# A gated feed-forward block in a transformer layer: seven products for four pairs of weight row tiles instead of three, two of the sums by accumulating transfers, activations through DRAM

## The chip, the cores and the metric

The kernel runs on one core of a Trainium2 chip. The metric is the device time of one execution in microseconds (us); lower is better. The time of the kernel before is the median of three runs.

## The reference, cut to what matters

One layer on 256 tokens of width 2048: a mixer of four head groups, then a gated feed-forward network of 5632 hidden columns. All arrays are float32.

```python
h = rms_norm(x, norm_mix_pre)
mix = hybrid_mixer(h, ...)
x = x + rms_norm(mix @ w_out, norm_mix_post)
h = rms_norm(x, norm_ffn_pre)
f = (silu(h @ w_gate) * (h @ w_up)) @ w_down
x = x + rms_norm(f, norm_ffn_post)
```

The change lies in `h @ w_gate` and `h @ w_up` (2048 x 5632 each) and in how the hidden activations reach `@ w_down`.

## The kernel before, in words

**Stages.** The input projections, the mixers and the output projection take the first 416 us. A stage for the first 512 columns of gate and up follows (the `gemm` call of L892, accumulators `ff`). Then a loop over ten *blocks* (L925) does the other 512-column slices of gate and up, and a last stage (from L946) does the down projection in two halves of 22 units. A kernel-wide library orders each engine's instructions by priority in the order of the code and by when it expects a buffer to be free; on the chip each engine works its own list strictly in that order and waits on semaphores.

**One float32 product is three matmuls.** A weight tile of 128 x 1024 (two pieces of 512 columns) is loaded into a buffer `raw`. ScalarE casts it to a rounded part `hi` (L768), and VectorE subtracts to get the rest, `lo` (L769); this is `split_to`, called by `split_new` (L799). `mm1` (L813) then issues three matmuls per product: activation times `hi`, activation times `lo`, activation remainder times `hi` (L815, L816, L817), each with 512 moving columns. There are five `raw` buffers and four each of `hi` and `lo`.

**A unit is two row tiles of the weights.** For a block, the 2048 rows are 16 row tiles, that is eight units `u` = 0 to 7. A unit's packed weights are four pieces: gate of row tile 0 (called a), up of row tile 0 (b), up of row tile 1 (d), gate of row tile 1 (c). `load4` (L786) loads pairs of them. With two halves of 128 tokens, a unit is a 2 x 2 by 2 x 2 block product: `eight` (L822) does it with eight products, of 3 matmuls each.

**`fifteen` (L833) does units u and u+1 together with 15 products:** seven for unit u by the scheme of Strassen and Winograd, and eight for u+1 in two parts of four (`part8`, L841). Seven products need sums of weights: `ta` = (a+b, d+b) by VectorE (L850), `tb` = (a+b+d, a+b+d+c) by two more adds (L855, L856), and sums of activations `cmb`, made once per unit before the loop (`combine_hs`, L884). The products go to four PSUM banks that hold the corrections (`m1`, `m6`, `m7`, `q5`) and four that hold results (`b2`, `b3`, `b4`, `b8`). Splits in the order in which they are made: a and d (w0), first half of u+1 (w0e), `ta` (wa), second half of u+1 (w1), c (wc), `tb` (wb). So `fifteen` makes five and a half splits of 1024 columns and three adds, where two calls of `eight` make four splits.

**A block before** is `eight` of unit 0, `fifteen` of units 1 and 2, 3 and 4, 5 and 6 (`S_UNITS`, L39), `sums` (L866), `eight` of unit 7: 8 + 15 + 15 + 15 + 8 = 61 products. `sums` combines the correction banks in SBUF tiles `g` and `v`: one copy on ScalarE (L868) and four adds on VectorE (L869 to L872). Then `turn` (L905) transposes the previous block's hidden activations on TensorE (8 transposes, accumulators `fT`, L911) and copies them to an SBUF tile `ft` (L912). `join` (L874) adds the result banks to `g` and `v` with four VectorE instructions (L876, L877, L879, L880). Last, ScalarE applies SiLU (L942) and VectorE multiplies gate by up (L943), two instructions each. Eleven `ft` tiles stay in SBUF until the down stage splits them (`hidden`, L914).

All loads are issued by the queue of SyncE (SP), in program order. The tiles `ta`, `tb`, `g`, `v`, `ft`, `cmb`, `hs` share one pool of 34 buffers of 4 KB per partition (tag `t`).

Of the kernel before, what the change touches and what calls it, by code (L numbers as in the profile page):

```python
# [10 lines left out]
F32 = mybir.dt.float32  # L11
# [27 lines left out]
S_UNITS = (1, 3, 5)  # L39
# [61 lines left out]
def block_kernel(ctx: ExitStack, tc: tile.TileContext, I, out):  # L101
# [655 lines left out]
    def spill(h):  # L757
        for q in range(2):
            nc.sync.dma_start(x_mid[:, 2 * h + q, :], xr[h][q])
# [73 lines left out]
    def fifteen(m, src, i, x, u, cmb, last, end=False):  # L833
# [69 lines left out]
    ft, fs, fcmb = [], {}, {}  # L903

    def turn(b, f):  # L905

        ft.append(T([P, 4, S], f"ft{b}"))
        for h in range(2):
# [3 lines left out]
            nc.scalar.copy(ft[b][:, :, h * P:(h + 1) * P], ps.rearrange("p (a b) -> p a b", a=4))  # L912

    def hidden(u):  # L914

        if u in fs:
            return
        v = ft[u // 2][:, 2 * (u % 2):2 * (u % 2) + 2, :]
        fs[u] = operand("fs", 2)[0]
        split_to(fs[u][:, :, 0, :], fs[u][:, :, 1, :], v)  # L920
        if u in S_DOWN[0] + S_DOWN[1]:
            fcmb[u] = combine(v)

    f = sg
    for b in range(1, FFB):  # L925
        m = {}
        g, v = T([P, 2, 512], "g"), T([P, 2, 512], "v")
        for u in range(KT // CK):
            i = (b - 1) * (KT // CK) + u
            if u in S_UNITS:  # L930
                fifteen(m, I["w_gu"], i, hs, u, cmb[u], u == S_UNITS[-1], u == KT // CK - 2)
            elif u - 1 not in S_UNITS:
                eight(m, I["w_gu"], i, hs, u, u == KT // CK - 1)
            if u == 4 and b == FFB - 1:
                hidden(0)
            if u == S_UNITS[-1]:
# [120 lines left out]
```

## Time and profile before

| what | value |
|---|---|
| median of three runs | 1135.75 us (1135.08 to 1139.37) |
| the profiled execution's own time | 1137.63 us |
| its span, first to last instruction | 1135.4 us |
| mean granted clock of TensorE | 0.996 of full |
| gate and up loop, ten blocks | from about 464.6 to 888.5 us of the span |
| down projection and end | from 888.5 us on |

A profile shows one execution: busy time of each engine, in what order instructions ran, what ended each wait, and what the DMA queues moved. A matmul's own duration is longer than the distance to the next one, since matmuls overlap; the distance is the price.

### The profile page before, as it was taken

To read this page: it belongs to the slowest core of one execution; us is meant where nothing else is said; L and a number is where in the kernel's file an instruction comes from. 1 tells how busy PE (TensorE), PEld (TensorE's weight loads), DVE (VectorE), ACT (ScalarE), POOL (GpSimd) and SP (SyncE) were. 2 spreads that over 40 slices of the span, in tenths; PEclk is the share of its full clock that TensorE was granted. 3 is DMA by queue.
4 is the path that set the end of the run, shared out by engine and by line. 5 is a ranking of instruction groups with operands and counts; after the bars stand their busy time and mean duration, and the time that the engine had idled before them with its cause. 6 is when DMAs were issued, how large, how long until landed. Compare 5 with 4: busy or idle time off the path is not lost.

```text
span 1135.4 us, 14600 instructions
## 1 busy us (share of the span) xinstructions
PE 1118.2 (98%) x5341; PEld 932.1 (82%) x5341; DVE 863.9 (76%) x1185; ACT 613.5 (54%) x846; POOL 14.2 (1%) x37
## 2 busy tenths in 40 slices
PE   9999999999999999999999999999999999999996
PEld 7787888888888887888888888888888788888885
DVE  6555647787565579688988988988988887778765
ACT  6644435565444556455555555555555665555542
POOL 0000000000000010000000000000000000000000
PEclk9999999999999999999999999999999999999999
DMA  8974454554556686466666666556556666666664
GB/s 276 326 231 149 131 160 129 196 186 157 158 183 194 199 314 223 137 197 204 190 200 209 192 192 214 189 190 220 186 188 222 188 189 198 201 206 208 206 218 149
DMA packets 75944, 224.36 MB, mean 198 GB/s; under 512 B 8032, under 2 KB 8544, under 8 KB 75872
## 3 DMA queue, kind: packets, MB, share of 16 engines
q1 hardware_dynamic: 75728, 223.42, 61.0%
q8 instruction: 42, 0.69, 0.2%
q14 instruction: 30, 0.25, 0.1%
q10 hardware_dynamic: 144, 0.01, 0.0%
HBM read 219.20 MB, written 4.19 MB: 197 GB/s over the span
## 4 chain that ended last, share of the span: by engine, by line
PE 91%; DVE 3%; DMA 3%; ACT 2%; issue 1%; POOL 0%; SPq 0%; DVEq 0%; POOLq 0%; ACTq 0%
PE b L815 15%; PE b L817 15%; PE b L816 15%; PE sx L223 3%; PE wo L197 3%; PE wo L198 3%; PE wo L200 3%; PE m L817 2%; PE m L815 2%; PE m L816 2%; PE dk L223 2%; PE lk L223 2%; PE rqk L223 2%; PE dq L223 2%; DMA raw<-in_w_in 2%; PE lq L223 1%
## 5 line engine op out<-in xcount | busy, mean ns | idle before, releaser
L768 ACT CAST hi<-raw 128x1024 fp32r<-128x1024 f32 x248 | 242.0, 983 | 173.6 <-PE b L817 143.6
L769 DVE TENSOR_TENSOR lo<-raw,hi 128x1024 fp32r<-128x1024 f32 x248 | 275.5, 1131 | 63.8 <-ACT hi L768 59.4
L183 DVE TENSOR_TENSOR lo<-raw,hi 128x1024 fp32r<-128x1024 f32 (+3 forms) x154 | 175.5, 1154 | 113.1 <-ACT hi L182 112.8
L182 ACT CAST hi<-raw 128x1024 fp32r<-128x1024 f32 (+3 forms) x154 | 150.6, 994 | 127.9 <-PE wo L200 32.1
L815 PE MATMUL b<-hi,hs 128*128 128x512 f32 x460 | 179.8, 391 | 0.0
L817 PE MATMUL b<-hi,hs 128*128 128x512 f32 x460 | 179.1, 389 | 0.0
L816 PE MATMUL b<-lo,hs 128*128 128x512 f32 x460 | 179.0, 389 | 0.0
L815 PE MATMUL b<-hi,fs 128*128 128x512 f32 x286 | 112.2, 392 | 1.8 <-ACT fs L768 1.8
L816 PE MATMUL b<-lo,fs 128*128 128x512 f32 x286 | 111.9, 391 | 0.0
L817 PE MATMUL b<-hi,fs 128*128 128x512 f32 x286 | 111.7, 391 | 0.0
L817 PEld LDWEIGHTS b<-hi,hs 128*128 128x128 f32 x460 | 86.3, 188 | 18.1
L816 PEld LDWEIGHTS b<-lo,hs 128*128 128x128 f32 x460 | 86.4, 188 | 17.7
L815 PEld LDWEIGHTS b<-hi,hs 128*128 128x128 f32 x460 | 86.4, 188 | 17.6
L768 ACT CAST hi<-tb 128x1024 fp32r<-128x1024 f32 x41 | 43.3, 1055 | 85.0 <-PE b L817 85.0
L769 DVE TENSOR_TENSOR lo<-tb,hi 128x1024 fp32r<-128x1024 f32 x41 | 50.0, 1220 | 31.6 <-ACT hi L768 31.3
L815 PEld LDWEIGHTS b<-hi,fs 128*128 128x128 f32 x286 | 54.0, 189 | 13.3 <-ACT fs L768 2.0
L816 PEld LDWEIGHTS b<-lo,fs 128*128 128x128 f32 x286 | 54.1, 189 | 11.4
L817 PEld LDWEIGHTS b<-hi,fs 128*128 128x128 f32 x286 | 54.1, 189 | 11.2
L768 ACT CAST hi<-ta 128x1024 fp32r<-128x1024 f32 x41 | 43.1, 1052 | 29.9 <-PE b L817 25.6
L769 DVE TENSOR_TENSOR lo<-ta,hi 128x1024 fp32r<-128x1024 f32 x41 | 49.9, 1217 | 6.1 <-ACT hi L768 6.0
L850 DVE TENSOR_TENSOR ta<-raw 128x1024 f32<-128x1024 f32 x41 | 49.9, 1216 | 4.3 <-DMA raw<-in_w_gu 4.1
L197 PE MATMUL wo<-hi,ms 128*128 128x512 f32 x128 | 50.0, 390 | 0.0
(378 smaller groups left out, 2017.7 us busy)
## 6 DMA issues: line engine op xcount, KB each, us to landing
raw<-in_w_gu SPq DMA_DIRECT2D x160, 512.0 KB, 4.7
raw<-in_w_down SPq DMA_DIRECT2D x88, 512.0 KB, 4.4
raw<-in_w_in SPq DMA_DIRECT2D x78, 512.0 KB, 4.6
raw<-in_w_out SPq DMA_DIRECT2D x32, 512.0 KB, 3.5
raw<-in_w_in SPq DMA_DIRECT2D x16, 384.0 KB, 3.1
raw<-in_w_g SPq DMA_DIRECT2D x8, 512.0 KB, 4.7
raw<-in_w_u SPq DMA_DIRECT2D x8, 512.0 KB, 4.6
raw<-in_w_in SPq DMA_DIRECT2D x8, 264.0 KB, 2.7
```

Source lines behind the costliest of these rows:

```text
L182: nc.scalar.copy(hi[:, k, :n], r3[:, k, :])
L183: nc.vector.tensor_tensor(lo[:, k, :n], r3[:, k, :], hi[:, k, :n].bitcast(F32), ALU.subtract)
L197: nc.tensor.matmul(d[:, :n], lhsT=a, rhs=hi[:, kt % CK, :n], start=first, stop=False)
L198: nc.tensor.matmul(d[:, :n], lhsT=a, rhs=lo[:, kt % CK, :n], start=False, stop=False)
L200: nc.tensor.matmul(d[:, :n], lhsT=b, rhs=hi[:, kt % CK, :n], start=False, stop=last)
L223: nc.tensor.matmul(o, lhsT=l, rhs=r, start=kt == 0 and i == 0, stop=kt == n_kt - 1 and i == 1)
L768: nc.scalar.copy(hi, v)
L769: nc.vector.tensor_tensor(lo, v, hi.bitcast(F32), ALU.subtract)
L815: nc.tensor.matmul(o, lhsT=xa, rhs=hi, start=first, stop=False)
L816: nc.tensor.matmul(o, lhsT=xa, rhs=lo, start=False, stop=False)
L817: nc.tensor.matmul(o, lhsT=xb, rhs=hi, start=False, stop=last)
L850: nc.vector.tensor_tensor(ta, ad, bc_[:, 0:1, :].to_broadcast([P, 2, 512]), ALU.add)
```

## The change

The change does five things.

1. `S_UNITS` becomes (0, 2, 4, 6): every block is four calls of `fifteen`, 60 products, and there is no call of `eight`. One more `cmb` is made before the loop.
2. For units 2 and 6 (`S_DMA`), `by_dma` makes `ta` by transfers: SP loads a and b into a buffer `ta`, then GpSimd's queue issues a transfer of b and d that adds to it. VectorE's add for `ta` goes away there. Since only a, d and c are then needed as such, the load of b and c becomes a load of c alone (256 KB).
3. In the block's last `fifteen`, the correction products come first, then `sums`, then the last four products of unit 7.
4. `turn` writes its transposed tile to a DRAM tensor `f_mid` by a transfer on ScalarE's queue, and `hidden` loads it back on SP and splits both units of it at once.
5. `spill`, which writes the residual to DRAM, is issued by ScalarE instead of SP.

```diff
-S_UNITS = (1, 3, 5)
+S_UNITS = (0, 2, 4, 6)
+S_DMA = (2, 6)
...
-            nc.sync.dma_start(x_mid[:, 2 * h + q, :], xr[h][q])
+            nc.scalar.dma_start(x_mid[:, 2 * h + q, :], xr[h][q])
...
+    def by_dma(src, i):
+        n = 4 * P * 512
+        w = src[i * n:(i + 1) * n].rearrange("(p c n) -> p c n", p=P, c=4)
+        t = T([P, 2, 512], "ta")
+        nc.sync.dma_start(t, w[:, 0:2, :])
+        nc.gpsimd.dma_start(t, w[:, 1:3, :], accum_op=ALU.add)
+        return t
...
-    def fifteen(m, src, i, x, u, cmb, last, end=False):
+    def fifteen(m, src, i, x, u, cmb, last, end=None, ta=None):
...
-        ad, bc_ = load4(src, i, slice(0, 3, 2), slice(1, 4, 2))
-        ta, tb = T([P, 2, 512], "ta"), T([P, 2, 512], "tb")
-        nc.vector.tensor_tensor(ta, ad, bc_[:, 0:1, :].to_broadcast([P, 2, 512]), ALU.add)
+        tb = T([P, 2, 512], "tb")
+        if ta is None:
+            ad, bc_ = load4(src, i, slice(0, 3, 2), slice(1, 4, 2))
+            c_ = bc_[:, 1:2, :]
+            ta = T([P, 2, 512], "ta")
+            nc.vector.tensor_tensor(ta, ad, bc_[:, 0:1, :].to_broadcast([P, 2, 512]), ALU.add)
+        else:
+            ad, c_ = load4(src, i, slice(0, 3, 2), slice(3, 4))
         r0, r1 = load4(src, i + 1, slice(0, 2), slice(2, 4))
         w0 = split_new(ad)
         prod(("m1", xpart(x, u, 0, 0), w0, 0), ("b3", s(3), w0, 1))
         w0e = split_new(r0)
         nc.vector.tensor_tensor(tb[:, 0, :], ta[:, 0, :], ad[:, 1, :], ALU.add)
-        nc.vector.tensor_tensor(tb[:, 1, :], tb[:, 0, :], bc_[:, 1, :], ALU.add)
-        part8(w0e)
+        nc.vector.tensor_tensor(tb[:, 1, :], tb[:, 0, :], c_[:, 0, :], ALU.add)
+        part8(0, w0e)
         wa = split_new(ta)
-        w1 = split_new(r1)
+        if end is None:
+            w1 = split_new(r1)
         prod(("q5", s(0), wa, 0), ("m7", s(2), wa, 1))
-        part8(w1)
-        wc = split_new(bc_[:, 1:2, :])
+        if end is None:
+            part8(1, w1)
+        wc = split_new(c_)
         wb = split_new(tb)
         prod(("b2", xpart(x, u, 1, 0), wc, 0), ("m6", s(1), wb, 0), ("b4", xpart(x, u, 1, 1), wb, 1))
+        if end is not None:
+            w1 = split_new(r1)
+            end()
+            part8(1, w1, True)
...
+    f_mid = dram.tile([P, FFB, 4, S], F32, name="f_mid")
...
+        nc.scalar.dma_start(f_mid[:, b], t)
...
+    def hidden(b):
+        t = T([P, 4, S], f"fl{b}")
+        nc.sync.dma_start(t, f_mid[:, b])
+        for k in range(2):
...
-        for u in range(KT // CK):
-            i = (b - 1) * (KT // CK) + u
-            if u in S_UNITS:
-                fifteen(m, I["w_gu"], i, hs, u, cmb[u], u == S_UNITS[-1], u == KT // CK - 2)
-            elif u - 1 not in S_UNITS:
-                eight(m, I["w_gu"], i, hs, u, u == KT // CK - 1)
+        i = (b - 1) * (KT // CK)
+        tas = {u: by_dma(I["w_gu"], i + u) for u in S_DMA}
+        for u in S_UNITS:
+            end = u == S_UNITS[-1]
+            fifteen(m, I["w_gu"], i + u, hs, u, cmb[u], end, (lambda: sums(m, g, v)) if end else None, tas.get(u))
...
-            for k in (u + 1, u + 2):
-                if k < n_u:
-                    hidden(k)
+            if q == 0 and u % 2 == 0 and u // 2 + 1 < FFB:
+                hidden(u // 2 + 1)
```

Three places in the instruction lists show what moved. The first is VectorE's list at the end of a block, from the first add of `sums` on (`lo<-raw,hi` is the subtraction of a split; `m`, `q` and `b` are the banks). Before:

```order
L869 TENSOR_TENSOR v_5275<-g_5274,m_182_5395 128x512
L769 TENSOR_TENSOR lo<-raw,hi 128x1024
L870 TENSOR_TENSOR g_5274<-v_5275,m_182_5368 128x512
L769 TENSOR_TENSOR lo<-raw,hi 128x1024
L871 TENSOR_TENSOR v_5275<-v_5275,q_182_5364 128x512
L872 TENSOR_TENSOR v_5275<-q_182_5364,g_5274 128x512
L876 TENSOR_TENSOR g_5274<-g_5274,b_180_5288 128x512
L877 TENSOR_TENSOR v_5275<-b_180_5292,v_5275 128x512
L879 TENSOR_TENSOR g_5274<-g_5274,b_180_5302 128x512
L880 TENSOR_TENSOR v_5275<-v_5275,b_180_5306 128x512
L850 TENSOR_TENSOR ta_5674<-raw 128x1024
L943 SCALAR_TENSOR_TENSOR v_5275<-v_5275,rsf_r,g_5274 128x512 x2
```

With the change (L890 to L893 are `sums`, L897 to L901 `join`, L965 the multiplication, L863 the add for `ta`, L770 the subtraction):

```order
L890 TENSOR_TENSOR v_5325<-g_5324,m_193_5415 128x512
L770 TENSOR_TENSOR lo<-raw,hi 128x1024
L891 TENSOR_TENSOR g_5324<-v_5325,m_193_5388 128x512
L897 TENSOR_TENSOR g_5324<-g_5324,b_193_5361 128x512
L892 TENSOR_TENSOR v_5325<-v_5325,q_193_5384 128x512
L893 TENSOR_TENSOR v_5325<-q_193_5384,g_5324 128x512
L898 TENSOR_TENSOR v_5325<-b_193_5351,v_5325 128x512
L900 TENSOR_TENSOR g_5324<-g_5324,b_193_5368 128x512
L901 TENSOR_TENSOR v_5325<-v_5325,b_193_5372 128x512
L965 SCALAR_TENSOR_TENSOR v_5325<-v_5325,rsf_r,g_5324 128x512 x2
L863 TENSOR_TENSOR ta_5704<-raw 128x1024
L870 TENSOR_TENSOR tb_5699<-ta_5704,raw 128x512
```

Both lists run through `sums`, `join` and the multiplication. Before, the next block's `ta` belongs to units 1 and 2; with the change it belongs to units 0 and 1, and the next split behind it is that of `ta`.

The second place is TensorE's list at the same boundary with the change, from the transposes on (L933; L816 to L818 are the three matmuls of a product):

```order
L933 MATMUL fT_127_5303<-ident,v_4591 128x128 x4
L933 MATMUL fT_128_5309<-ident,v_4591 128x128 x4
L816 MATMUL m_193_5347<-hi,hs_3717 128x512
L817 MATMUL m_193_5347<-lo,hs_3717 128x512
L818 MATMUL m_193_5347<-hi,hs_3717 128x512
L816 MATMUL b_193_5351<-hi,cmb_4059 128x512
L817 MATMUL b_193_5351<-lo,cmb_4059 128x512
L818 MATMUL b_193_5351<-hi,cmb_4059 128x512
L816 MATMUL b_193_5351<-hi,hs_3718 128x512
L817 MATMUL b_193_5351<-lo,hs_3718 128x512
L816 MATMUL b_193_5361<-hi,hs_3718 128x512
L817 MATMUL b_193_5361<-lo,hs_3718 128x512
```

After the transposes come `m1` and `b3` of unit 0 and four products of unit 1, 18 matmuls in all, and then the first matmul that reads `hi` of `ta`. Before, 24 matmuls of unit 0 stand behind the transposes, then 18 of units 1 and 2, and only then the first that reads `hi` of `ta`.

The third is SP's list with the change, around the loads into `ta` for the DMA sums (L839; `ta` number 5326 is unit 2's, 5329 unit 6's of one block):

```order
L796 DMA raw<-in_w_gu 128x1024 x2
L796 DMA raw<-in_w_gu 128x2x512 x2
L796 DMA raw<-in_w_gu 128x1024 x2
L796 DMA raw<-in_w_gu 128x2x512
L796 DMA raw<-in_w_gu 128x512
L839 DMA ta_5326<-in_w_gu 128x1024
L839 DMA ta_5329<-in_w_gu 128x1024
L796 DMA raw<-in_w_gu 128x1024 x2
L796 DMA raw<-in_w_gu 128x2x512 x2
```

The code asks for both at the start of the block. They stand behind five and a half loads of the block: all four of units 0 and 1, and the loads of a, d and of c of unit 2.

## Rows read from the trace of the kernel before

**Rows 1.** the page, busy time of each engine, and the granted clock in 40 slices

```profile
PE 1118.2 (98%) x5341; PEld 932.1 (82%) x5341; DVE 863.9 (76%) x1185; ACT 613.5 (54%) x846; POOL 14.2 (1%) x37
PEclk9999999999999999999999999999999999999999
```

**Rows 2.** the chain that ended last: start us, length us, what (transposes between blocks)

```profile
506.15 0.87 PE fT L911 x8
548.53 0.87 PE fT L911 x8
...
887.65 0.87 PE fT L911 x8
```

**Rows 3.** busy time by stretch; columns by engine, then clock, DMA share, GB/s

```profile
core 0: us, PE busy (x) PEld busy (x) DVE busy (x) ACT busy (x) POOL busy (x), PEclk, DMA share, GB/s
591.80:634.18 42.38, 42.38 (x193) 35.18 (x192) 37.86 (x46) 24.19 (x28) 0.00 (x0) 1.00 0.63 198
```

**Rows 4.** TensorE in order of time at a block boundary: start us, us, what

```profile
590.77 1.03 PE L911 MATMUL fT<-ident,v 128*128 128x128 f32 x8
591.56 0.48 PE L815 MATMUL b<-hi,hs 128*128 128x512 f32 x1
591.88 0.40 PE L816 MATMUL b<-lo,hs 128*128 128x512 f32 x1
592.11 0.39 PE L817 MATMUL b<-hi,hs 128*128 128x512 f32 x1
```

**Rows 5.** VectorE in order of time at two boundaries, same columns

```profile
593.90 1.41 DVE L943 SCALAR_TENSOR_TENSOR v<-v,rsf_r,g 128x512 f32<-128x512 f32 x2
595.23 2.35 DVE L769 TENSOR_TENSOR lo<-raw,hi 128x1024 fp32r<-128x1024 f32 x2
...
628.08 0.68 DVE L869 TENSOR_TENSOR v<-g,m 128x512 f32<-128x512 f32 x1
628.68 1.22 DVE L769 TENSOR_TENSOR lo<-raw,hi 128x1024 fp32r<-128x1024 f32 x1
629.82 0.68 DVE L870 TENSOR_TENSOR g<-v,m 128x512 f32<-128x512 f32 x1
...
634.54 0.68 DVE L880 TENSOR_TENSOR v<-v,b 128x512 f32<-128x512 f32 x1
635.14 1.22 DVE L850 TENSOR_TENSOR ta<-raw 128x1024 f32<-128x1024 f32 x1
```

**Rows 6.** group by line, three blocks: count, busy us, mean ns, idle before

```profile
L768 ACT CAST hi<-ta 128x1024 fp32r<-128x1024 f32 x9 | 9.5, 1052 | 5.3 <-PE b L817 5.3
```

**Rows 7.** VectorE later in the block: idle time before a row and its releaser

```profile
622.87 1.23 DVE L769 TENSOR_TENSOR lo<-tb,hi 128x1024 fp32r<-128x1024 f32 x1 [2.02 <-ACT hi L768]
626.94 1.23 DVE L769 TENSOR_TENSOR lo<-raw,hi 128x1024 fp32r<-128x1024 f32 x1 [1.49 <-ACT hi L768]
```

**Rows 8.** TensorE after its two longest waits before the last stage

```profile
38.33 0.39 PE L223 MATMUL lq<-xs,lo 128*128 128x256 f32 x1 [2.01 <-DVE lo L183]
896.68 0.50 PE L815 MATMUL b<-hi,fs 128*128 128x512 f32 x1 [1.80 <-ACT fs L768]
898.24 0.63 PE L815 MATMUL b<-hi,fs 128*128 128x512 f32 x1
...
901.23 0.52 PE L816 MATMUL b<-lo,fs 128*128 128x512 f32 x1
```

**Rows 9.** stretches behind those two waits, columns as in rows 3

```profile
38.00:40.00 2.00, 1.67 (x10) 1.49 (x11) 1.24 (x2) 1.26 (x3) 0.00 (x0) 1.00 0.74 223
898.00:900.00 2.00, 2.00 (x7) 1.50 (x6) 2.00 (x4) 1.23 (x3) 0.00 (x0) 0.52 0.87 307
```

**Rows 10.** the page, DMA issues: transfer, queue, count, size, us to landing

```profile
raw<-in_w_gu SPq DMA_DIRECT2D x160, 512.0 KB, 4.7
x_mid<-xr SPq DMA_DIRECT2D x4, 512.0 KB, 7.0
```

More of the change, by code (lines that the diff above doesn't have):

```diff
@@ L839, in prod, with part8 @@
                 mm1(m, name, xa, xb, hi[:, k, :], lo[:, k, :], last and name[0] != "b")
-        def part8(w):
-            k = 0 if w is w0e else 1
+        def part8(k, w, fin=False):
             for h in range(2):
@@ L845, in part8 @@
                 for j in range(2):
-                    mm1(m, names[j ^ k], *xpart(x, u + 1, k, h), w[0][:, j, :], w[1][:, j, :], end and k == 1)
-        ad, bc_ = load4(src, i, slice(0, 3, 2), slice(1, 4, 2))
-        ta, tb = T([P, 2, 512], "ta"), T([P, 2, 512], "tb")
-        nc.vector.tensor_tensor(ta, ad, bc_[:, 0:1, :].to_broadcast([P, 2, 512]), ALU.add)
+                    mm1(m, names[j ^ k], *xpart(x, u + 1, k, h), w[0][:, j, :], w[1][:, j, :], fin)
+        tb = T([P, 2, 512], "tb")
[6 more added lines that the diff above has]
+            ad, c_ = load4(src, i, slice(0, 3, 2), slice(3, 4))
         r0, r1 = load4(src, i + 1, slice(0, 2), slice(2, 4))
@@ L901, in block_kernel @@
         nc.vector.scalar_tensor_tensor(sg[h], accs[h][1], rs_f[h][:, 0:1], sg[h], ALU.mult, ALU.mult)
-    ft, fs, fcmb = [], {}, {}
+    fs, fcmb = {}, {}
+    f_mid = dram.tile([P, FFB, 4, S], F32, name="f_mid")
     def turn(b, f):
-        ft.append(T([P, 4, S], f"ft{b}"))
+        t = T([P, 4, S], f"ft{b}")
         for h in range(2):
@@ L911, in turn @@
                 nc.tensor.transpose(ps[:, j * P:(j + 1) * P], f[h][:, j * P:(j + 1) * P], ident)
[L912 to L922, printed above, removed]
+            nc.scalar.copy(t[:, :, h * P:(h + 1) * P], ps.rearrange("p (a b) -> p a b", a=4))
+        nc.scalar.dma_start(f_mid[:, b], t)
[3 more added lines that the diff above has]
+        for k in range(2):
+            u = 2 * b + k
+            v = t[:, 2 * k:2 * k + 2, :]
+            fs[u] = operand("fs", 2)[0]
+            split_to(fs[u][:, :, 0, :], fs[u][:, :, 1, :], v)
+            if u in S_DOWN[0] + S_DOWN[1]:
+                fcmb[u] = combine(v)
     f = sg
@@ L927, in block_kernel @@
         g, v = T([P, 2, 512], "g"), T([P, 2, 512], "v")
-        for u in range(KT // CK):
-            i = (b - 1) * (KT // CK) + u
-            if u in S_UNITS:
-                fifteen(m, I["w_gu"], i, hs, u, cmb[u], u == S_UNITS[-1], u == KT // CK - 2)
-            elif u - 1 not in S_UNITS:
-                eight(m, I["w_gu"], i, hs, u, u == KT // CK - 1)
+        i = (b - 1) * (KT // CK)
[3 more added lines that the diff above has]
+            fifteen(m, I["w_gu"], i + u, hs, u, cmb[u], end, (lambda: sums(m, g, v)) if end else None, tas.get(u))
             if u == 4 and b == FFB - 1:
                 hidden(0)
-            if u == S_UNITS[-1]:
-                sums(m, g, v)
         turn(b - 1, f)
```

## Prediction

> **What bounds the kernel now.** I read the page first: TensorE is busy 98% of the span at full clock, VectorE 76% [rows 1]. Then the chain of waits. In the gate and up loop it is TensorE alone, and its transposes, one set per block, come at an even step: 506.15 and 887.65 are the first and the last of ten, so a block takes 381.5 / 9 = 42.39 us [rows 2]. Next, busy time by block: TensorE has no idle time, VectorE works 37.86 of 42.38 us, and the DMA engines are busy 0.63 of the time at 198 GB/s [rows 3]. A block holds 61 x 3 = 183 matmuls and the transposes (0.87 us), so a matmul costs (42.39 - 0.87) / 183 = 0.227 us. So a product less is worth time only if nothing makes TensorE wait. What decides is therefore the order of VectorE at the block boundary, read from the timeline [rows 4, 5]. VectorE waits for ScalarE's casts late in a block, up to 2.02 us at a time [rows 7]: it is ahead there and has slack. At the boundary it has none.
>
> **What the change saves.** One product per block: 3 x 0.227 = 0.68 us, times ten blocks **-6.8 us**.
>
> **What it adds on VectorE.** Per block one add for `ta` less (three become two; 1.14 us is the step from one 1024-column row to the next, 628.68 to 629.82 [rows 5]), two adds for `tb` more (0.60 us each, the step of 512 columns, 634.54 to 635.14 [rows 5]), and 22 splits for 20.5. That is -1.14 + 1.20 + 1.71 = +1.8 us. VectorE then works about 39.6 of 41.7 us. As a sum this still fits, so I cost it at nothing by itself; its cover is TensorE's 41.7 us, and if that went, all 1.8 us a block would show.
>
> **The block boundary, step by step.** Take as zero the start of the transposes. With the change TensorE has behind them 18 matmuls whose operands are split before the boundary. Transposes 0.79 us (590.77 to 591.56 [rows 4]) plus 18 x 0.227 plus 0.09 for the slow first one makes 4.95 us of cover. The next matmul reads `hi` of `ta`.
>
> When is that ready? Backwards from zero there are 21 matmuls (c and `tb` nine, unit 7's last four products twelve) behind the last product that reads `ta` of unit 6. That product ends at -21 x 0.227 + 0.16 = -4.6 us (0.16: a matmul runs 0.39 and steps 0.227 [rows 4]). Its `hi` buffer is the one that the next block's first cast needs, as there are four and three splits lie between. So: cast 1.06 us [rows 6] to -3.5, its subtraction 1.14 to -2.35. Only now does VectorE reach `sums`. Its list, each entry by its step: `sums` and `join` 8 x 0.60, one subtraction among them 1.14, the two of the multiplication 1.33 (593.90 to 595.23), the add for `ta` 1.22 [rows 5]. Sum 8.5: `ta` is there at 6.15 us. Its cast ends at 7.2, with hand-overs of some 0.06 each at about 7.4. **TensorE waits 7.4 - 4.95 = 2.45 us.** Then five matmuls read `hi` parts only, but one of them needs the cast behind (8.4 us): 0.5 us more. Together 2.95 us. Before, 42 matmuls lie between the transposes and the first read of `ta`, 9.5 us of cover, and nothing waits.
>
> There are nine such boundaries (into blocks 2 to 10): 9 x 2.95 = **+26.5 us**. The first block starts behind the stage before, without this queue of adds.
>
> **The clock.** Rows show that a wait of TensorE can cost twice. After a wait of 1.80 us it ran from 898.24 to 901.23 with seven steps of 0.43 us [rows 8], at a granted clock of 0.52, the 1.2 GHz level [rows 9]: some eight matmuls lost 0.2 us each, 1.6 us. It had run without a wait before. After a wait of 2.01 us at 36 us the clock stayed at 1.00, 2.4 GHz [rows 8, 9]. So one wait in two. Bounds: 0 and 9 x 1.6 = 14.4 us. The waits here are longer, so I take six of nine: **+9.6 us**.
>
> **The transfers into `ta`.** SP can issue the load of c of unit 2 when a `raw` buffer comes free, by my count the one whose subtraction lies between the first two adds of `sums`, which ends at -0.6 us; the two loads into `ta` follow at about 0. A load of 512 KB lands in 4.7 us [rows 10]. VectorE wants unit 2's `ta` for `tb`, behind the two `tb` adds and the splits of `ta`, of unit 1's second half, of c and `tb` and of unit 2's first: from 7.4 us 4 x 1.14 + 0.60, near 12.7. That leaves 8.0 us for the accumulating transfer. No row shows one. Lower bound: as a plain load, 4.7 us, no wait. Upper: a load and a store in sequence, 4.7 + 7.0 = 11.7 us [rows 10], a wait of 3.7 us in each of ten blocks, +37 us. I take the lower, since it is the same 512 KB from the same tensor.
> The Trainium skill (DMA: Bandwidth & Descriptors, section on the anatomy of a DMA on the GpSimd path) gives 2.0 us plus the bytes at 436 GB/s, an estimate of 3.2 us; by it nothing waits either.
>
> These transfers also share the DMA engines. A block moves 16 pieces of 512 KB now; with the change 14 + 1 (two halves of c), two plain and two accumulating loads and the `f_mid` store, 20, or 22 if accumulating counts twice. Busy share 0.63 x 20/16 x 42.4/45.3 = 0.74, up to 0.81. Loads will land later. VectorE runs without slack for the first half of a block, so a late load there shows. Bounds 0 and, with the upper bound above, inside the same 37 us; I take 0.5 us a block: **+5 us**.
>
> **At nothing, or nearly.** The 11 stores and loads through `f_mid` are spread under TensorE's work; the store's issue is on ScalarE, which is busy 24 of 42 us [rows 3]. `spill` moves four issues to ScalarE once. The down stage keeps its instruction counts; at its start TensorE waits 1.80 us already [rows 8], and splitting two units at once lengthens that: **+1 us**.
>
> **Sum:** -6.8 + 26.5 + 9.6 + 5 + 1 = +35.3 us. The profiled execution took 1137.63 us (span 1135.4, 2.2 us around it), 1.9 above the median of 1135.75. From it the sum gives 1172.9, against the median **1171 us**.
>
> **The rivals.**
> - *The boundary wait alone* (clock stays up, loads in time): -6.8 + 26.5 + 1 = +20.7, 1156 us. For it: the clock stayed up after 2.01 us.
> - *The accumulating transfers are late* and VectorE stands at unit 2's `tb` in each block. Price up to 37 us besides the boundary's, in place of the 5: it decides from 8.0 us issue to landing on. 1185 to 1210 us. For it: a store takes 7.0 us, the transfer must read what it changes, and loads queue behind it. The Trainium skill (the same page, on issuing engines not being separate DMA queues) speaks for this one: transfers from every queue run on the same 16 engines, so a sum moved off VectorE is paid there. No run here shows it yet.
> - *The boundary is covered* and the product is gained: 1129 us. Place: VectorE's queue of `sums`, `join` and `ta`. It decides from `ta`'s cast being done 4.95 us after the transposes start, 2.45 us earlier than I count. For it: before, VectorE is ahead at the end of a block [rows 7]. Against: its list is worked strictly in order, and the adds of `join` wait for TensorE's last products.
> - *Gain and wait cancel*: a boundary wait of 0.7 us instead of 2.95. Within 5 us of before.
>
> **How the numbers follow.** Forecast 0.46, boundary alone 0.20, late transfers 0.27, covered 0.04, cancelled 0.03. A measurement of this kernel tells about 0.5%, 5.7 us, from no change: covered is faster (0.04), cancelled the same (0.03), the rest slower (0.93). The range reaches from just under the boundary alone, 1152, into the late transfers, 1205; it leaves out the two small cases and the upper end of the late transfers.
>
> **What would show it.** A step between transposes of about 45 to 47 us. In the timeline, TensorE idle 2 to 3 us behind 18 matmuls after the transposes, released by ScalarE's cast of `ta`. Granted clock of about half in some stretches behind it. VectorE without idle time until mid-block. In the DMA issues, the accumulating transfer under 8 us and no wait of VectorE on it; a long wait of `tb` on a DMA into `ta` would mean late transfers. I am wrong if TensorE shows no wait at the boundary, or if the loss lies in the down stage.

## The result and the profile after

The changed kernel takes **1179.27 us** (median of four runs, 1175.02 to 1180.65), the kernel before 1136.46 us beside it: ratio **1.0376, interval 1.0357 to 1.0394**. The forecast was 1171 us in a range of 1152 to 1205. The profiled execution is the shortest of the four, 1175.02 us with a span of 1173.2 us, so what its trace shows (37.8 us more span than before) is a little less than what the medians differ by.

The page first: busy times, the queue of the accumulating transfers, the shares of the chain that ended last, and the DMA issues (transfer, queue, count, size, us to landing).

```profile
PE 1128.5 (96%) x5311; PEld 928.1 (79%) x5311; DVE 888.3 (76%) x1221; ACT 629.7 (54%) x867; POOL 31.9 (3%) x57
...
q0 software_dynamic: 2880, 10.49, 5.0%
...
PE 73%; DVE 12%; DMA 8%; ACT 3%; issue 3%; POOL 0%; DVEq 0%; SPq 0%; POOLq 0%; ACTq 0%
...
raw<-in_w_gu SPq DMA_DIRECT2D x140, 512.0 KB, 4.6
...
ta<-in_w_gu SPq DMA_DIRECT2D x20, 512.0 KB, 5.9
ta<-in_w_gu POOLq DMA_DIRECT2D x20, 512.0 KB, 7.8
...
f_mid<-ft ACTq DMA_DIRECT2D x11, 512.0 KB, 6.1
```

TensorE falls from 98% to 96% [rows 1], and the chain now runs 12% over VectorE and 8% over transfers. Where? The transposes (line 933 now), first and tenth set:

```profile
504.76 0.49 PE L933 MATMUL fT<-ident,sg 128*128 128x128 f32 x3
...
923.74 0.71 PE L933 MATMUL fT<-ident,v 128*128 128x128 f32 x5
```

Nine blocks take 418.98 us, 46.55 each in place of 42.39 [rows 2]: +37.5 us. Ahead of the first transposes it is 1.2 us less, behind the last 1.5 us more. The loss lies in the blocks.

The first of the ten blocks has no such boundary ahead of it. From its first matmul to the transposes it takes 40.81 us (463.95 to 504.76), and 41.49 before (464.51 to 505.99). So there the saved product shows at once, 0.68 us:

```profile
463.95 0.39 PE L816 MATMUL m<-hi,hs 128*128 128x512 f32 x1
```

```profile
464.51 0.39 PE L815 MATMUL b<-hi,hs 128*128 128x512 f32 x1
...
505.99 0.49 PE L911 MATMUL fT<-ident,sg 128*128 128x128 f32 x3
```

One boundary in order of time, TensorE, then VectorE and ScalarE (lines 816 to 818 are the three matmuls of a product, 769 the cast, 770 its subtraction, 863 the add that makes `ta`, 965 the multiplication that closes a block; square brackets: idle before, and what ended it). The transposes start at 551.14.

```profile
555.94 0.40 PE L818 MATMUL b<-hi,hs 128*128 128x512 f32 x1
558.40 0.51 PE L816 MATMUL q<-hi,cmb 128*128 128x512 f32 x1 [2.06 <-ACT hi L769]
558.74 0.39 PE L816 MATMUL m<-hi,cmb 128*128 128x512 f32 x1
559.35 0.98 PE L816 MATMUL b<-hi,hs 128*128 128x512 f32 x3 [0.22 <-ACT hi L769]
```

```profile
554.12 0.68 DVE L901 TENSOR_TENSOR v<-v,b 128x512 f32<-128x512 f32 x1
554.72 1.41 DVE L965 SCALAR_TENSOR_TENSOR v<-v,rsf_r,g 128x512 f32<-128x512 f32 x2
556.05 1.22 DVE L863 TENSOR_TENSOR ta<-raw 128x1024 f32<-128x1024 f32 x1
...
557.30 1.05 ACT L769 CAST hi<-ta 128x1024 fp32r<-128x1024 f32 x1 [2.33 <-DVE ta L863]
```

This is the queue that the prediction counted: `join`, multiplication, `ta`, cast. VectorE's rows follow each other without a hole, and TensorE stands 2.46 us from start to start where a step is 0.23. Before, VectorE went from the multiplication to the remainder of a cast and nobody waited [rows 4, 5].

The waits (who, line, for whom: us in total, times, longest) and two blocks as stretches (columns as in [rows 3]), with 2 us of the second:

```profile
ACT hi L769 <- DMA raw<-in_w_gu: 28.6, 13, 4.7
...
PE q L816 <- ACT hi L769: 18.8, 9, 2.1
...
DVE tb L870 <- DMA ta<-in_w_gu: 7.6, 3, 5.8
```

```profile
551.14:598.10 46.96, 43.56 (x189) 34.15 (x188) 39.39 (x46) 25.54 (x29) 1.74 (x2) 1.00 0.72 224
598.10:644.02 45.92, 43.80 (x189) 35.43 (x188) 39.48 (x46) 25.75 (x29) 1.74 (x2) 0.96 0.73 229
606.00:608.00 2.00, 1.97 (x5) 1.40 (x5) 2.00 (x3) 1.72 (x3) 0.87 (x1) 0.50 0.97 182
```

Nine waits of TensorE at nine boundaries. VectorE waits for a sum made by a transfer three times, but 5.8 of the 7.6 us are one wait in the first block, where nothing is lost. And two blocks lose time in different ways: the second runs a while at half clock (0.50, the 1.2 GHz level) behind its boundary; the first doesn't, and still takes 1 us more. The chain of waits through the first one says what binds there instead:

```profile
556.13 1.14 DVE ta L863
558.64 2.36 DVE lo L770 x2
561.02 8.10 DMA raw<-in_w_gu
570.30 1.84 DVE lo L770 x2
572.15 4.98 DMA raw<-in_w_gu
577.83 1.23 DVE lo L770
```

Half a block hangs on VectorE and on loads, one of which takes 8.10 us where the median was 4.7 [rows 10]; in the kernel before it hung on TensorE alone. Six of the nine blocks have such a load in the chain, of 7.1 to 8.9 us. So there are two suspects, the boundary's queue and the transfers, and their waits lie in the same half block. That is what the experiments had to take apart.

### The profile page after: what moved, and what is told of

Read it like the earlier page. It is cut to its first block, busy times and chain, and to the rows that moved or that the text cites. A ratio compares the mean times of both kernels' runs of the same rounds, so it can differ in the third digit from the quotient of the medians.

```text
span 1173.2 us, 14714 instructions
## 1 busy us (share of the span) xinstructions
PE 1128.5 (96%) x5311; PEld 928.1 (79%) x5311; DVE 888.3 (76%) x1221; ACT 629.7 (54%) x867; POOL 31.9 (3%) x57
## 4 chain that ended last, share of the span: by engine, by line
PE 73%; DVE 12%; DMA 8%; ACT 3%; issue 3%; POOL 0%; DVEq 0%; SPq 0%; POOLq 0%; ACTq 0%
PE b L817 10%; PE b L816 10%; PE b L818 10%; DMA raw<-in_w_gu 6%; DVE lo L770 4%; PE sx L224 3%; PE wo L201 2%; PE wo L198 2%; PE wo L199 2%; PE m L817 2%; PE dk L224 2%; PE m L818 2%; PE m L816 2%; PE lk L224 2%; PE rqk L224 2%
## 5 line engine op out<-in xcount | busy, mean ns | idle before, releaser
L770 DVE TENSOR_TENSOR lo<-raw,hi 128x1024 fp32r<-128x1024 f32 x248 | 271.3, 1111 | 77.8 <-ACT hi L769 73.4
L769 ACT CAST hi<-raw 128x1024 fp32r<-128x1024 f32 x248 | 235.0, 963 | 172.2 <-PE b L818 107.1
L817 PE MATMUL b<-lo,hs 128*128 128x512 f32 x400 | 158.1, 395 | 4.2 <-DVE lo L770 3.9
L816 PE MATMUL b<-hi,hs 128*128 128x512 f32 x400 | 157.1, 401 | 3.0 <-ACT hi L769 3.0
L818 PE MATMUL b<-hi,hs 128*128 128x512 f32 x400 | 155.0, 391 | 0.0
L816 PE MATMUL b<-hi,fs 128*128 128x512 f32 x286 | 111.3, 393 | 3.2 <-ACT fs L769 3.2
L818 PE MATMUL b<-hi,fs 128*128 128x512 f32 x286 | 111.0, 390 | 0.0
L817 PEld LDWEIGHTS b<-lo,hs 128*128 128x128 f32 x400 | 75.8, 189 | 25.0 <-DVE lo L770 9.5
L816 PEld LDWEIGHTS b<-hi,hs 128*128 128x128 f32 x400 | 75.8, 191 | 23.7 <-ACT hi L769 7.7
L818 PEld LDWEIGHTS b<-hi,hs 128*128 128x128 f32 x400 | 75.5, 189 | 15.6
L769 ACT CAST hi<-tb 128x1024 fp32r<-128x1024 f32 x51 | 53.7, 1052 | 52.9 <-PE b L818 36.2
L770 DVE TENSOR_TENSOR lo<-tb,hi 128x1024 fp32r<-128x1024 f32 x51 | 62.3, 1221 | 17.7 <-ACT hi L769 17.6
L769 ACT CAST hi<-ta 128x1024 fp32r<-128x1024 f32 x51 | 53.5, 1049 | 32.5 <-DVE ta L863 25.6
L770 DVE TENSOR_TENSOR lo<-ta,hi 128x1024 fp32r<-128x1024 f32 x51 | 62.2, 1219 | 5.8 <-ACT hi L769 5.8
L816 PEld LDWEIGHTS b<-hi,fs 128*128 128x128 f32 x286 | 54.1, 189 | 15.1 <-ACT fs L769 3.6
L818 PEld LDWEIGHTS b<-hi,fs 128*128 128x128 f32 x286 | 54.0, 189 | 11.5 <-DVE fs L770 0.2
L198 PE MATMUL wo<-hi,ms 128*128 128x512 f32 x128 | 50.0, 390 | 0.0
L201 PE MATMUL wo<-hi,ms 128*128 128x512 f32 x128 | 49.8, 389 | 0.0
```

The lines of the kernel that those rows point to most:

```text
L198: nc.tensor.matmul(d[:, :n], lhsT=a, rhs=hi[:, kt % CK, :n], start=first, stop=False)
L201: nc.tensor.matmul(d[:, :n], lhsT=b, rhs=hi[:, kt % CK, :n], start=False, stop=last)
L769: nc.scalar.copy(hi, v)
L770: nc.vector.tensor_tensor(lo, v, hi.bitcast(F32), ALU.subtract)
L816: nc.tensor.matmul(o, lhsT=xa, rhs=hi, start=first, stop=False)
L817: nc.tensor.matmul(o, lhsT=xa, rhs=lo, start=False, stop=False)
```

## The experiments

Prices are medians against the kernel before, measured beside each group of runs (1136.2 to 1136.8 us), with the ratio's interval. "Boundary theory" is the prediction's main term, "transfer theory" its rival; the "third theory" is that each hides the other.

**1. No accumulating transfer.**

```diff
-S_DMA = (2, 6)
+S_DMA = ()
```

> No pair's a+b, b+d is made by a transfer; VectorE makes all four (two adds of 1.22 us more in a block, 38.6 + 2.4 us of 42). Boundary theory (the loss is the cast of ta behind VectorE's ends of the block, 2.1 to 2.5 us idle in each block, and the half clock after it): the idle time at the boundary stays 2.0 to 2.6 us, and the time goes down by no more than the 5 us of the transfers' term, 1170 to 1180 us. Transfer theory (the loss is loads that come late beside the accumulating transfers, 1.1 to 1.9 us of waits at some 15 and 26 us after the transposes): these mid-block waits go, the step falls from 46.6 to 44 to 45 us, 1155 to 1165 us. Third theory (VectorE is behind from the boundary to the middle of the block, and what the one wait doesn't cost the other does): the mid-block waits shrink, half of it comes back at the boundary by the clock, 1160 to 1172 us.

Measured 1170.25 us, ratio 1.0298 (1.0281 to 1.0315): 9.0 us of the 42.8 come back. Two of its blocks as stretches:

```profile
555.34:600.64 45.30, 42.64 (x189) 34.32 (x188) 41.39 (x47) 25.86 (x29) 0.00 (x0) 1.00 0.57 198
600.64:647.05 46.41, 44.13 (x189) 35.33 (x188) 41.77 (x48) 25.86 (x29) 0.00 (x0) 0.96 0.56 193
```

and its waits at the boundary:

```profile
PE q L816 <- ACT hi L769: 18.8, 9, 2.1
```

The boundary's nine waits are what they were, to the digit. The transfer theory's step of 44 to 45 us is missed. The boundary theory's range holds, but it allowed no more than 5 us to come back; the third theory's range holds the time too, so this run alone doesn't decide between the two. Here the half clock is visible by itself: five blocks without it take 45.30 to 45.35 us, four with it 46.15 to 46.63, **1.05 us for a stretch at half clock**.

**2. `ta` of the block's first pair on GpSimd**, transfers kept.

```diff
-            nc.vector.tensor_tensor(ta, ad, bc_[:, 0:1, :].to_broadcast([P, 2, 512]), ALU.add)
+            (nc.gpsimd if u == 0 else nc.vector).tensor_tensor(ta, ad, bc_[:, 0:1, :].to_broadcast([P, 2, 512]), ALU.add)
```

> The add that makes ta of the block's first pair goes from VectorE to GpSimd, which is idle there; accumulating transfers stay. It can then run beside the joins. No row has GpSimd's time for 128x1024 elements; up to some 4 us it should still end before VectorE reached it. Boundary theory: idle time at the boundary falls from 2.1 to 2.5 us to under 1 us, most half-clock stretches go, and some 25 us of the 37 come back, 1140 to 1155 us. Transfer theory: no change, 1174 to 1181 us. Third theory: the boundary's idle time goes, the mid-block waits on lo and tb grow by as much, step within 0.7 us of 46.6, 1170 to 1181 us.

Measured 1172.19 us, 1.0322 (1.0296 to 1.0347). The boundary's wait is gone (at most 0.55 us is left) and the clock never halves there, yet the step is 45.5 to 47.0. As numbers this is the third theory. But the edit had a price of its own, which the sixth run made plain: see there.

**3. Both edits.**

```diff
-S_DMA = (2, 6)
+S_DMA = ()
...
-            nc.vector.tensor_tensor(ta, ad, bc_[:, 0:1, :].to_broadcast([P, 2, 512]), ALU.add)
+            (nc.gpsimd if u == 0 else nc.vector).tensor_tensor(ta, ad, bc_[:, 0:1, :].to_broadcast([P, 2, 512]), ALU.add)
```

> Both edits: ta of the first pair on GpSimd, the other three on VectorE, no accumulating transfer. Boundary theory: as with the GpSimd edit alone, within 6 us of it, 1137 to 1155 us. Transfer theory: as without accumulating transfers, within 6 us of it. Third theory: far more than the sum of the two single edits, a step of 43 to 43.7 us, 1140 to 1150 us.

Measured 1147.33 us, 1.0093 (1.0078 to 1.0108), a step of 43.10 to 43.13 us in every block. Alone the edits gave 9 and 7 us, together 32: the two losses do overlap.

**4. All adds for `ta` and `tb` on GpSimd**, no transfer.

```diff
-S_DMA = (2, 6)
+S_DMA = ()
...
-            nc.vector.tensor_tensor(ta, ad, bc_[:, 0:1, :].to_broadcast([P, 2, 512]), ALU.add)
+            nc.gpsimd.tensor_tensor(ta, ad, bc_[:, 0:1, :].to_broadcast([P, 2, 512]), ALU.add)
...
-        nc.vector.tensor_tensor(tb[:, 0, :], ta[:, 0, :], ad[:, 1, :], ALU.add)
-        nc.vector.tensor_tensor(tb[:, 1, :], tb[:, 0, :], c_[:, 0, :], ALU.add)
+        nc.gpsimd.tensor_tensor(tb[:, 0, :], ta[:, 0, :], ad[:, 1, :], ALU.add)
+        nc.gpsimd.tensor_tensor(tb[:, 1, :], tb[:, 0, :], c_[:, 0, :], ALU.add)
```

> All adds that make ta and tb go to GpSimd, no accumulating transfer; VectorE keeps casts' remainders and the block's end, some 31 us of a 42 us block. If VectorE's queue is what both waits come from, PE waits nowhere over 1 us in a block, the step is 41.7 to 42.5 us, and the time 1129 to 1138 us, at or below the kernel before (1136). If loads or the clock bind by themselves, the step stays over 43.5 us. If GpSimd's adds take longer than some 3 us each or slow VectorE's own, tb comes late and the step is over 45 us.

Measured 1226.19 us, 1.0776 (1.0738 to 1.0814). The groups by line (count, busy us, mean ns, idle before):

```profile
L863 POOL TENSOR_TENSOR ta<-raw 128x1024 f32<-128x1024 f32 x51 | 133.5, 2619 | 407.9 <-DMA raw<-in_w_gu 238.5 <-DMA raw<-in_w_down 92.6 <-ACT wd01j L984 41.0
L871 POOL TENSOR_TENSOR tb<-tb,raw 128x512 f32<-128x512 f32 x51 | 104.5, 2049 | 4.0
...
L770 DVE TENSOR_TENSOR lo<-tb,hi 128x1024 fp32r<-128x1024 f32 x51 | 101.8, 1997 | 26.6 <-ACT hi L769 26.5
```

GpSimd needs 2.6 and 2.0 us for what VectorE does in 1.22 and 0.68, and VectorE's own subtraction beside it takes 2.00 us in place of 1.22 on the mean. The last clause of the expectation was the right one: VectorE is not relieved, it is held up. In a block it is now busy 47 to 48 us with 35 instructions, where in run 1 it was busy 41.4 us with 47.

**5. The block's end late.** The third run's kernel, and the SiLU and the multiplication of a block are given inside the next block's second pair.

```diff
+        part8(0, w0e)
+        if rest is not None:
+            rest()
...
-        for h in range(2):
-            nc.scalar.activation(g[:, h, :], g[:, h, :], AF.Silu, scale=rs_f[h][:, 0:1])
-            nc.vector.scalar_tensor_tensor(v[:, h, :], v[:, h, :], rs_f[h][:, 0:1], g[:, h, :], ALU.mult, ALU.mult)
+        def rest(g=g, v=v):
+            for h in range(2):
+                nc.scalar.activation(g[:, h, :], g[:, h, :], AF.Silu, scale=rs_f[h][:, 0:1])
+                nc.vector.scalar_tensor_tensor(v[:, h, :], v[:, h, :], rs_f[h][:, 0:1], g[:, h, :], ALU.mult, ALU.mult)
```

> The third run's kernel (1147.3 us, step 43.11), and the two SiLU activations and two multiplies that close a block are given to the engines inside the next block's second pair instead of ahead of its first pair. If PE's last waits in the block (0.55 us at a b product 5.2 us and 0.93 us at an m product 7.6 us after the transposes, start to start) come from VectorE's and ScalarE's ends of the block standing ahead of the first pair's tb and casts, both go: the step becomes 41.7 to 42.0 us, some 11 us less in nine blocks, 1134 to 1138 us. If VectorE is short over the whole block (its busy time 38 to 39 us of 43) the 1.33 us of multiplies is only waited for later: step 42.8 or more, 1144 to 1148 us.

Measured 1135.51 us, 0.9994 (0.9985 to 1.0003): level with the kernel before. The step is 41.87 to 42.45 us, not quite the 41.7 to 42.0 expected. One block:

```profile
594.20:636.30 42.10, 42.10 (x189) 34.42 (x188) 41.64 (x46) 25.55 (x30) 2.40 (x1) 1.00 0.60 211
```

TensorE has no idle time here, and VectorE works 41.64 of 42.10 us. Each of the two expectations is half right: the end of the block was the wait, and with it gone VectorE is full.

**6. The same with the turned activations resident in SBUF**, with `turn` and `hidden` as in the kernel before.

```diff
-        nc.scalar.dma_start(f_mid[:, b], t)
...
-        t = T([P, 4, S], f"fl{b}")
-        nc.sync.dma_start(t, f_mid[:, b])
+        v = ft[u // 2][:, 2 * (u % 2):2 * (u % 2) + 2, :]
```

> As the kernel with the late block ends, and the turned activations stay in SBUF as in the kernel before (no store to DRAM, no load in the down stage); only the residual's spill stays on ScalarE's queue. If the load of the second group from DRAM is what PE waits 3.06 us for at the start of the down stage (1.80 us in the kernel before), that wait falls back to some 1.8 us and the time is 2 to 5 us below the kernel with the late ends: 1130 to 1134 us, below the kernel before. If the detour through DRAM is hidden, the two are within 1 us.

Measured 1136.54 us, 1.0002 (0.9990 to 1.0013): no gain, a miss. The wait at the down stage's start did fall, to 1.80 us, but the second to the fifth of the nine steps went up to 42.5 to 42.7 us. In the four blocks ahead of them VectorE has four combinations for the down stage to make, which need no load now and had been placed there (`cs<-ft` at 621.75 is one); I take these for the cause, since TensorE then waits 0.2 us for VectorE early in the next block. More telling are two rows that start together, of GpSimd and VectorE:

```profile
625.59 2.40 POOL L863 TENSOR_TENSOR ta<-raw 128x1024 f32<-128x1024 f32 x1 [40.29 <-DVE lo L770]
...
625.80 3.26 DVE L770 TENSOR_TENSOR lo<-tb,hi 128x1024 fp32r<-128x1024 f32 x1 [0.31 <-ACT hi L769]
```

The subtraction takes 3.26 us where it takes 1.22 without an add beside it; nine of run 6's 299 subtractions of this size take 2.9 to 3.3 us, each beside one of GpSimd's adds. By these times VectorE stood until GpSimd's add was over. It is the same in the second run:

```profile
589.74 2.47 POOL L863 TENSOR_TENSOR ta<-raw 128x1024 f32<-128x1024 f32 x1 [27.92 <-DMA raw<-in_w_gu]
...
589.87 2.90 DVE L770 TENSOR_TENSOR lo<-raw,hi 128x512 fp32r<-128x512 f32 x1
```

2.90 us for 0.68. So an add given to GpSimd saved VectorE 1.14 us (its step) and cost it 2.04 or 2.2. The Trainium skill (SBUF — State Buffer, section "Who interferes with whom") says that a VectorE instruction with two SBUF inputs contends with a GpSimd instruction that reads SBUF; these rows agree. It also means that the second run did not test the boundary alone.

**7. The detour through DRAM alone**, on the kernel before.

```diff
-            nc.sync.dma_start(x_mid[:, 2 * h + q, :], xr[h][q])
+            nc.scalar.dma_start(x_mid[:, 2 * h + q, :], xr[h][q])
...
+        nc.scalar.dma_start(f_mid[:, b], t)
...
+        t = T([P, 4, S], f"fl{b}")
+        nc.sync.dma_start(t, f_mid[:, b])
```

> The kernel before with only the detour: turned activations stored to DRAM from ScalarE's queue and loaded in the down stage, the residual's spill on ScalarE's queue; three pairs by seven products as before. Block step 42.4 us as before. If the detour costs what the start of the down stage shows in the third run (1.3 us more after the last transposes, and a longer half-clock stretch), 1137 to 1140 us; if it is hidden, 1135 to 1137 us.

Measured 1140.58 us, 1.0042 (1.0025 to 1.0058): **3.8 us**, just over what was expected. The block step is 42.37 to 42.41 as before. What is longer is the start of the down stage: TensorE in order of time there, then ScalarE's wait, then SP's queue:

```profile
907.88 0.79 PE L815 MATMUL b<-hi,fs 128*128 128x512 f32 x1 [5.16 <-ACT fs L768]
```

```profile
ACT fs L768 <- DMA fl<-f_mid: 4.8, 1, 4.8
```

```profile
893.11 4.59 SPq L795 DMA_DIRECT2D raw<-in_w_down  x3
897.76 0.42 SPq L919 DMA_DIRECT2D fl<-f_mid  x1
```

5.16 us of waiting where there were 1.80 [rows 8]. The cast waits for a load from `f_mid`, which SP issues at 897.76, behind three weight loads, and which lands only some 9.4 us later. How much of that is its place in the queue and how much the other transfers in flight was not tried apart. This profile is of the slowest of six executions (1144.32 us); in the change's own profile the same wait is 3.2 us.

**8. Plain loads into `ta`, without the accumulating transfer**, on the second run's kernel. The sums a+b and b+d of units 2 and 6 are left out by this, so the result is not the layer's; only the time counts.

```diff
-        nc.gpsimd.dma_start(t, w[:, 1:3, :], accum_op=ALU.add)
```

> The second run's kernel (ta of the first pair on GpSimd, 1172 us) with the accumulating transfer left out: only the plain load of a and b into ta stays, so that the products of pairs 2 and 6 that read ta and tb work on a and b in place of a+b and b+d. If the accumulating transfers themselves (their 512 KB each, their landing 7.8 us after issue, and the loads that come late beside them) cost what lies between the second and the third run (25 us), this is 1143 to 1150 us. If the extra plain load and its place ahead of the block's loads in SP's queue cost it, it stays at 1165 to 1173 us.

Measured 1147.56 us, 1.0099 (1.0084 to 1.0114), the third run's time. The plain loads cost nothing; the accumulating transfers cost all of the 25 us between runs 2 and 3.

**9. An early front in place of GpSimd.** VectorE makes the next block's first `ta` ahead of the sums that close a block; the rest as in run 6, and the down stage's casts kept in their place.

```diff
+    def front(src, i):
+        ad, bc_ = load4(src, i, slice(0, 3, 2), slice(1, 4, 2))
+        ta = T([P, 2, 512], "ta")
+        nc.vector.tensor_tensor(ta, ad, bc_[:, 0:1, :].to_broadcast([P, 2, 512]), ALU.add)
+        return ad, bc_[:, 1:2, :], ta
...
+        if nxt is not None:
+            nxt()
         if end is not None:
             w1 = split_new(r1)
             end()
```

> As the kernel with late block ends and resident activations (1136.5 us), but no add on GpSimd: VectorE makes ta of the next block's first pair ahead of the sums that close a block, and the casts and combinations for the down stage are kept out of the blocks. No accumulating transfer. If GpSimd's add holds VectorE up while it runs (a cast's remainder took 3.26 us beside it, 1.21 without), VectorE gains 2.05 - 1.14 = 0.9 us a block, the step falls from 42.1 to 42.7 us to 41.7 to 42.1 us, 1131 to 1135 us. If VectorE is full all the same (41.7 us busy of 42.0), the step stays at 42.1 to 42.6 us, 1135 to 1139 us.

Measured **1131.00 us, 0.9957 (0.9946 to 0.9969)**: 0.4% faster than the kernel before, and far faster than the change. VectorE around the boundary at 632.84 (line 852 is the early add, 879 the first `tb` add), and two blocks:

```profile
625.16 1.23 DVE L852 TENSOR_TENSOR ta<-raw 128x1024 f32<-128x1024 f32 x1 [0.23 <-DMA raw<-in_w_gu]
626.30 1.22 DVE L770 TENSOR_TENSOR lo<-tb,hi 128x1024 fp32r<-128x1024 f32 x1
...
635.83 0.68 DVE L914 TENSOR_TENSOR v<-v,b 128x512 f32<-128x512 f32 x1
636.43 0.68 DVE L879 TENSOR_TENSOR tb<-ta,raw 128x512 f32<-128x512 f32 x1
```

```profile
591.01:632.84 41.83, 41.83 (x189) 34.54 (x188) 40.93 (x47) 25.57 (x29) 0.00 (x0) 1.00 0.59 201
632.84:674.65 41.81, 41.81 (x189) 34.53 (x188) 40.81 (x47) 25.53 (x29) 0.00 (x0) 1.00 0.61 202
```

The same add on the same engine, 7.7 us before the boundary and not 4.9 us behind it, costs the chain behind it nothing: VectorE comes to `sums` 2.3 us ahead of the boundary, as in the change. TensorE waits nowhere in a block, the step is 41.79 to 41.85 us, and at last the saved product shows at every step: 0.57 us a block under the 42.39 of before. The late ends of run 5 are in this kernel as well; the early add without them was not run.

**10, 11 and 12: transfers again**, with the boundary cleared this way: one accumulating transfer a block for the pair at unit 4, the change's two at 2 and 6, two at 4 and 6. One line each:

```diff
-S_DMA = ()
+S_DMA = (4,)
```

> As the kernel with the early front, and the third pair's (unit 4) a+b, b+d by one accumulating transfer in each block, started as in the change at the block's start; wanted some 20 us later. VectorE does 1.14 us less in a block. If what the transfers cost (25 us between the second and third run) is that the second pair's sum lands after VectorE comes to it, this one costs nothing and the time is 0 to 4 us below the kernel without, 1129 to 1134 us. If it is loads that come late beside any accumulating transfer, half of the 25 us shows, 1142 to 1148 us.

> The kernel with the early front, with the change's two accumulating transfers, for the pairs at units 2 and 6. Boundary relieved without GpSimd, so this tells whether the second run's missing gain was GpSimd's. Late-landing theory: PE waits 2 to 3.4 us at some 15 us after the transposes, step 44.7 to 45.5 us, 1158 to 1168 us. Boundary theory of the prediction (transfers 5 us at most): 1133 to 1140 us.

> The same with two accumulating transfers, at units 4 and 6: as many bytes and issues as in the change, only not for the block's second pair. Late-landing theory: most of what the transfers at 2 and 6 cost comes back, step 41.7 to 42.7 us, 1130 to 1141 us. If their bytes or their slowing of loads cost it: as at 2 and 6, 1155 us or more.

Measured: 1132.69 us, 0.9967 (0.9954 to 0.9979), for one at 4; 1149.38, 1.0113 (1.0098 to 1.0128), for 2 and 6; 1140.07, 1.0036 (1.0026 to 1.0047), for 4 and 6. Against run 9: 1.7 us more with intervals that overlap; **+18.4 us**; +9.1 us. The waits of the run with 2 and 6 and its accumulating transfers among the page's DMA issues, then the same of the run with 4 and 6:

```profile
ACT hi L769 <- DMA raw<-in_w_gu: 29.9, 11, 3.5
DVE tb L879 <- DMA ta<-in_w_gu: 26.1, 10, 6.1
...
PE b L822 <- DVE lo L770: 11.1, 11, 1.7
```

```profile
ta<-in_w_gu POOLq DMA_DIRECT2D x20, 512.0 KB, 8.4
```

```profile
ACT hi L769 <- DMA raw<-in_w_gu: 44.4, 23, 4.3
...
PE b L821 <- ACT hi L769: 5.0, 6, 1.1
```

```profile
ta<-in_w_gu POOLq DMA_DIRECT2D x20, 512.0 KB, 9.4
```

With 2 and 6, VectorE waits ten times for the second pair's sum, 26.1 us. With 4 and 6 it waits for no sum at all; what is left are weight loads that come late beside two transfers (casts wait for them 44.4 us, in run 9 once for 0.9). With one, the transfer lands after 6.3 us at the median; casts wait 17.1 us in all for loads, but none of it reaches TensorE (the nine steps take 376.36 us, as in run 9). So by the difference late landing is about half of the 18 us (9.3 come back by moving the first transfer from the second pair to the third), and loads slowed by two transfers at once are the other half. In runs 11 and 12 the second transfer of a block is issued within some 3 us of the first, though its sum is wanted much later; two transfers further apart were not tried. Run 10 also shows that there was nothing to win: VectorE is 1.14 us a block less busy and the time is the same, since TensorE had no wait to lose.

Run 11 missed the late-landing theory's 1158 to 1168 us, on the low side. And it corrects the second run: the change's two transfers were in both, the boundary cleared in both, 1172 and 1149 us. The 22.8 us between them are GpSimd's hold on VectorE, the ends of the block and the DRAM detour; I did not split them further. "Each hides the other" is true to a smaller extent: taking the transfers away is worth 9.0 us with the boundary's wait there (the intervals leave some 3 us either way) and 18.4 without.

## Why the prediction came out, and where its terms were off

The forecast (slower, the boundary's queue as the main cause, half clock behind it) holds. Of what was to show it, these did: a step of 45.9 to 47.6 us (45 to 47 foretold), TensorE idle 2.06 to 2.13 us behind 18 matmuls after the transposes, released by the cast of `ta`, at all nine boundaries (the next matmul starts 2.46 - 0.23 = 2.2 us later than it could; 2.45 counted), half clock at five of nine (six foretold), an accumulating transfer under 8 us (7.8 at the median). Two did so in part: VectorE is without idle time until some 12 us behind the transposes, not until mid-block, and then waits for casts whose loads come late; and it does wait for a sum made by a transfer, in two of the nine blocks, 1.8 us in all.

Term by term. The runs make a ladder from the change to run 9 and on to before, so its parts add up by construction, but for the detour, which was priced on the kernel before. The traces give the same ladder in the nine steps between transposes: 418.98 us in the change, 412.04 in run 1, 376.36 in run 9, 381.50 before.

- *The saved product*, -6.8 us. Measured where nothing else stands in the way: run 9 against before, -5.2 us; by the traces -5.1 in the nine steps and -0.7 in the first block. Right, nearly whole.
- *The boundary*, +26.5 us, and *the clock*, +9.6 us: 36.1 together. Run 1 against run 9, less 3.8 us for the detour: 35.5 us, and 35.7 in the nine steps of the traces. Run 9 differs from run 1 by the early add and the late ends together, so this is the price of the whole queue at the boundary and not of the one add. Inside, the shares were different. A block of run 1 at full clock is 3.5 us over run 9's (45.3 against 41.8), where 2.95 were counted; among what was not in the count is 0.38 us of idle time at the next `m` product, behind the same queue. A stretch at half clock cost 1.05 us, not the 1.6 read from [rows 8]; most of the difference is that wait at the next `m` product (0.55 us from start to start), which three of the four blocks with half clock don't have. In the change itself it cost nothing that can be seen: the five blocks with it average 46.4 us, the four without 46.8 (46.5 without the last, which also makes splits for the down stage), since VectorE and the loads set the pace there in the chain shown above. There the boundary's two waits are 2.2 and 0.4 us from start to start, 2.6 us where 2.95 were counted. The other 2.1 us by which a step exceeds run 9's are half clock in some blocks and late loads in others, so that the trace of the change alone can't price the clock.
- *The shared transfers*, +5 us: the mis-sized term. Measured 9.0 us in the change (6.9 in the nine steps of the traces) and 18.4 with the boundary cleared. The step that failed is "I take 0.5 us a block" for loads that land later: it stood on no row, and beside two accumulating transfers the loads in the chain took 7.1 to 8.9 us where 4.7 was the median. "I take the lower, since it is the same 512 KB from the same tensor" was wrong in size too: an accumulating transfer landed 7.8 us after its issue at the median, and the plain load into the same tile ahead of it took 5.9. That did little harm in the change, because unit 2's own transfer landed after 5.7 to 7.6 us, under the 8.0 from which the prediction has VectorE wait. The Trainium skill's estimate of 3.2 us (DMA: Bandwidth & Descriptors, anatomy of a DMA on the GpSimd path) is less than half of the 7.8. Its rule that issuing engines are not separate queues agrees with loads slowed beside the transfers. The rival of late transfers, with VectorE standing at unit 2's `tb` in each block, is not what the change did (two blocks of nine, 1.8 us); it shows in run 11, where VectorE is no longer late itself and waits ten times. Its upper end of 1210 us is also 7 us above what its terms add up to (35.3 - 5 + 37 on 1135.75).
- *The detour through DRAM*, +1 us: 3.8 on the kernel before. In the change's own trace all that lies behind the last transposes is 1.5 us longer, so 3.8 is rather too much for it there. The wait is for a load that leaves late behind weight loads on SP's queue and lands late, a queue that the step did not consider. That "splitting two units at once" costs anything is not shown.
- *VectorE's 1.8 us more a block at nothing*: right as a sum while something else waits (run 1 makes two adds more and still wins), and right in its condition: in run 5, with the waits gone, 41.64 of 42.10 us of VectorE are what is left.

So the sum was 7.5 us low (35.3 against 42.8). By the medians most of that lies with transfers: 4.0 for the accumulating ones and 2.8 for the detour; the saved product gave 1.6 less, and the boundary with its clock was 0.6 too high (7.8 together, since the groups of runs have slightly different medians of the kernel before). The profiled execution of the change is 4 to 6 us shorter than the other three, and its trace is only 2.5 us above the sum (37.8 against 35.3). Where the longer ones lose the rest no trace shows, so the shares of the miss are less sure than its main term.

## What to carry to other kernels

A block of work that ends in a chain on one engine needs, at its start, work whose operands that chain doesn't touch. Count the cover in matmuls, and if it is short, move the one add that opens the next block ahead of the chain and the block's last steps behind it. Without the transfers, that turned 45.8 us a block (run 1) into 41.8 (run 9); with that add on GpSimd instead it was 42.2 (run 5), and with the two transfers besides 43.9 (run 11). When two waits lie in the same stretch, undoing one shows little; price each with the other removed. A transfer that sums is not a load of the same size: ask when it can start, when it is wanted, and what it travels beside.

## What the runs showed of the hardware that I had not expected

- A GpSimd add of 128x1024 f32 takes 2.4 to 2.9 us at the medians of the runs, and in runs 2 and 6 the VectorE subtraction that starts beside it takes 2.9 to 3.3 us in place of 0.68 or 1.22: the two do not run together. Work given to GpSimd was paid by VectorE with interest (run 4 takes 56 us more than run 1, which makes the same adds on VectorE).
- One accumulating transfer of 512 KB a block landed in 6.3 us at the median and cost nothing; two, issued within 5 us of each other, landed in 7.8 to 9.4 us at the medians and cost 9 us even where no one waited for their sums.
- Nine waits of TensorE of 2.1 us, all alike: the clock fell behind five of them (in run 1, behind four), to the 1.2 GHz level, and stayed up behind the others.
